# Gate rows ahead of the attention's operands, retention chunks behind it, and more buffers for the merge and the output weight

## The chip, the cores and the metric

The kernel runs on one NeuronCore of a Trainium2 chip. The metric is the device time of one execution in microseconds (us); lower is better. A profile shows one execution with the start, the length and the releaser of each instruction on TensorE (PE), VectorE (DVE), ScalarE (ACT), GpSimd (POOL) and the DMA queue of SyncE (SP).

## The reference

One step of a decoder layer: sparse attention (an indexer picks up to 256 keys for each token) beside multi-scale retention, both gated and merged, for 1024 tokens of a prompt and 32 tokens of eight sampled sequences (4 each). All arithmetic is in float32. What matters here comes behind the projection `u = h @ w_in`:

```python
y_a = attn_fn(qa, ka, va, qi, ki, wi) * silu(za)          # 1056 x 512
y_r = group_norm_heads(ret) * g_ret * silu(zr)            # 1056 x 512
merged = sigmoid(ga) * (y_a @ w_pa) + sigmoid(gr) * (y_r @ w_pr)   # 1056 x 1024
x = x + gate[:, None, :] * (merged @ w_out)               # 1056 x 1024
y = rms_norm(x, g_final)
```
The outputs are y, the new rows of keys, values and indexer keys, and the retention states.

## The kernel before

The arrays are held with channels on the partitions and tokens along the row: a row tile is 128 channels by TT = 1056 tokens (1024 prompt, 32 sample). To keep float32 precision each product of a big matrix is done as three matmuls, high part by high part, high by low and low by high. `parts` splits a row: ACT copies it to the high part (L829) and DVE takes the difference as the low part (L830). A weight is split in the same way by `wsplit` (ACT `wh` L194, DVE or POOL `wl` L195).

The projection, the indexer and the choice of keys fill the first 830 us. What follows goes in four stages.

1. *Retention's inputs and the gates* (to 855): `rows_in` reads the four rows of y_r back from the DRAM tensor YR by way of a buffer `u` and splits them into `rh`, `rl`. The gates, as tanh rows in DRAM (TG: rows 0 to 1023 for the attention, 1024 to 2047 for the retention; (1 + tanh)/2 is the sigmoid), are finished.
2. *Attention of the prompt, with the retention's product beside it* (855 to 1025). There are 16 steps: four pairs of heads `p`, two groups of blocks of 128 tokens, two halves. `pair_operands` loads a pair's q, kh, kl (twelve loads of 64 rows, two heads), V and za. `logits` makes a step's logits (L1055, L1056) and the softmax (DVE L1057, ACT L1062, POOL L1064); `turn` transposes the weights (L1077, copies L1079); `combine` multiplies by V (L1094) and, with every second step, scales by za and splits into `yah`, `yal`. Step s + 2's logits are made behind step s's combination. Beside it `from_retention(j)` yields, for each block j of 128 output channels (0 to 7), three *chunks* c of 352 tokens: 12 matmuls each (4 blocks of 128 input channels by 3), written in one bank of PSUM (`out_weights`, L875 to L877). `use_r` scales a chunk by its gate row `u` (L1118). After the third chunk the row is stored to the DRAM tensor RT (L1120). The list `side` holds all 24 chunks; 9 are drawn at the first step and one at each of the others.
3. *Merge* (1025 to 1077). For each j the gate row `t` (from TG, L1172) and the retention's row `u` (from RT, L1173) are loaded; 12 matmuls for each of three chunks of `yah`, `yal` by `w_pa`; `use_a` scales by the gate (DVE L1176), adds the retention (POOL L1177) and splits the sum into MH and ML (the last 32 tokens into MS). The tile's release on DVE frees the bank for a later chunk; there are four banks (`pj`, bufs=4). After every second j, `load_wo` loads 128 columns of the first half of `w_out` into `wst` (L1163), ACT writes the high part `woh` (L1165), POOL or DVE the low part `wol` (L1166).
4. *Output* (1077 to the end). The other half of `w_out` is loaded in the same way in a pool `op_` that opens when the merge's rows are closed, and the product MH, ML by WO goes over nine tiles of tokens with two halves of columns (L1215 to L1225), followed by the gate, the residual and the norm.

Engines work off their instructions in order. The program's text gives the order only roughly: a scheduler with a model of the times (`schedule_with_timeline_sim=True`) places the instructions on each engine, and `tc.issue_after(x)` keeps the instructions inside it from being placed ahead of x. Almost all transfers are issued by SP, in its order: a transfer that waits holds the ones behind it. A tile's buffers are given round robin: with bufs=2 the third tile of a name waits until the users of the first are done. Pools whose memory overlaps that of a closed pool wait for that pool's last users as well (`reuse_waits="tile"`: tile by tile); `side="right"` allots from the other end of SBUF.

Of the kernel before, what the change touches and what calls it, by code (L numbers as in the profile page):

```python
# [2 lines left out]

# [5 lines left out]
F32 = mybir.dt.float32  # L9
# [4 lines left out]
OP = mybir.AluOpType  # L14
# [4 lines left out]
D = 1024  # L19
T = 1024  # L20
NB, NI = 8, 4
NS = NB * NI
TT = T + NS
CH = TT // 3
KT = D // 128
# [94 lines left out]
def _hybrid_step(ctx, tc, A, outs, dbg):  # L120
    nc = tc.nc
    f32 = lambda ap: ap.bitcast(F32)

    cst = ctx.enter_context(tc.tile_pool(name="cst", bufs=1, reuse_waits="tile"))
    dram = ctx.enter_context(tc.tile_pool(name="scr", bufs=1, space=DRAM))
    wp_ = ExitStack()
    wp = wp_.enter_context(tc.tile_pool(name="wp", bufs=2, side="right", reuse_waits="tile"))
    selp = ctx.enter_context(tc.tile_pool(name="selp", bufs=1, reuse_waits="tile"))
    hs_ = ExitStack()
    hp = hs_.enter_context(tc.tile_pool(name="hp", bufs=1, reuse_waits="tile", side="right"))  # L130
    ps1 = ExitStack()
# [268 lines left out]
    TG = dram.tile([2 * D, TT], F32, name="TG")  # L400
# [180 lines left out]
    with ExitStack() as s1:  # L581
# [4 lines left out]
        with ExitStack() as s2:  # L586
# [35 lines left out]
            for g in range(3):  # L622
                p = pt().rearrange("p (t c) -> p t c", c=128)
                for t in range(4 * g, min(4 * g + 4, 9)):
                    n = 128 if t < 8 else NS
# [11 lines left out]
            for b in range(7, 1, -1):  # L637
                W = (b + 1) * 128
                for h in range(4):
                    p = pl()  # L640
# [30 lines left out]
            for G in (0, 1):  # L671
                p = pt()[:, :128]
                nc.tensor.matmul(p, SX[:NS, 128 * G:128 * G + 128], dw.rearrange("p h t -> p (h t)"), start=True, stop=True)
                t = ip.tile([128, 4, NS], F32, name="wt", bufs=2)
# [4 lines left out]
            for G in (0, 1):  # L679
                KP = []  # L680
                for b in range(4 * G, 4 * G + 4):
# [5 lines left out]
                    p = pt()  # L687
# [5 lines left out]
                x, xn = pl(), pt()  # L693
# [12 lines left out]
            x, xn = pl(), pt()  # L706
# [120 lines left out]
    def parts(dst, src):  # L827

        nc.scalar.copy(dst[0], src)  # L829
        nc.vector.tensor_sub(dst[1], src, f32(dst[0]))  # L830
# [37 lines left out]
    def out_weights(src, use, j, kt, rows_h, rows_l):  # L868

        wh, wl = wsplit(wq, wload(wq, src, 128 * j, 128, kt), 128, kt)  # L870
        for c in range(3):
            x = pj()[:, :CH]
            sl = slice(c * CH, c * CH + CH)
            for k in range(kt):
                nc.tensor.matmul(x, wh[:, k], rows_h[:, k, sl], start=(k == 0), stop=False)  # L875
                nc.tensor.matmul(x, wh[:, k], rows_l[:, k, sl], start=False, stop=False)  # L876
                nc.tensor.matmul(x, wl[:, k], rows_h[:, k, sl], start=False, stop=(k == kt - 1))  # L877
            use(c, sl, x)
            yield

    def rows_in(pool, src):
        hi, lo = [pool.tile([128, 4, TT], F32R, name=n) for n in ("rh", "rl")]
        for k in range(4):
            t = pool.tile([128, TT], F32, name="u", bufs=2)
            nc.sync.dma_start(t, src[128 * k:128 * k + 128])
            parts((hi[:, k], lo[:, k]), t)
        return hi, lo
# [101 lines left out]
    for p in range(4):  # L989
        x = tl.tile([128, TT], F32, name="kx", bufs=1)  # L990
        split_rows(tl, O_KA + 128 * p, p, KD, ks, x)
        token_rows(tl, x, p, k_out, ks_out, None)
    for p in range(4):
        x = tl.tile([128, TT], F32, name="raw", bufs=2)
# [8 lines left out]
    rm = rm_.enter_context(tc.tile_pool(name="rm", bufs=1, reuse_waits="tile"))  # L1003
# [12 lines left out]
    yah, yal = [yp.tile([128, 4, TT], F32R, name=n) for n in ("yah", "yal")]  # L1016
# [24 lines left out]
    def logits(ap, step):  # L1041

        blocks, ops = step["blocks"], step["ops"][0]
        lg = step["lg"] = ap.tile([128, 2, 9 * 128], F32, name="lg", bufs=3)
        c0 = 0
        for b in blocks:
            W = (b + 1) * 128
            for i, (q, kh, kl) in enumerate(ops):
                l = lg[:, i, c0:c0 + W]
                st = ap.tile([128, 4], F32, name="st", bufs=12)  # L1050
                qb = q[:, b * 128:b * 128 + 128]
                for n0 in range(0, W, 512):
                    n1 = min(W, n0 + 512)
                    x = pbank("lg", 2)
                    nc.tensor.matmul(x[:, :n1 - n0], qb, kh[:, n0:n1], start=True, stop=False)  # L1055
                    nc.tensor.matmul(x[:, :n1 - n0], qb, kl[:, n0:n1], start=False, stop=True)  # L1056
                    nc.vector.tensor_tensor_reduce(  # L1057
                        out=l[:, n0:n1], in0=x[:, :n1 - n0], in1=BI[b][:, n0:n1], scale=1.0,
                        scalar=BIGNEG if n0 == 0 else st[:, 0:1], op0=OP.add, op1=OP.max,
                        accum_out=st[:, 0:1] if n1 < W else st[:, 1:2])  # L1060
                nc.vector.tensor_scalar(st[:, 2:3], st[:, 1:2], -0.125, None, op0=OP.mult)  # L1061
                nc.scalar.activation(l, l, AF.Exp, bias=st[:, 2:3], scale=0.125, accum_out=st[:, 3:4])  # L1062
                nc.vector.reciprocal(st[:, 0:1], st[:, 3:4])  # L1063
                nc.gpsimd.tensor_scalar(l, l, st[:, 0:1], 0.5, op0=OP.mult, op1=OP.mult)  # L1064
            c0 += W
# [37 lines left out]
    RT = dram.tile([D, TT], F32, name="RT")  # L1103
    with ExitStack() as s4:
        ap = s4.enter_context(tc.tile_pool(name="ap", bufs=1, side="right", reuse_waits="tile"))
        loaded = {}

        def operands(p):
            if p not in loaded:
                loaded[p] = pair_operands(ap, p)  # L1110
            return loaded[p]

        def from_retention(j):
            u = rm.tile([128, TT], F32, name="u", bufs=2)
            nc.sync.dma_start(u, TG[D + 128 * j:D + 128 * j + 128])

            def use_r(c, sl, x):
                nc.vector.scalar_tensor_tensor(u[:, sl], u[:, sl], 1.0, x, op0=OP.add, op1=OP.mult)  # L1118
            yield from out_weights(A["w_pr"][0], use_r, j, 4, yrh, yrl)
            nc.sync.dma_start(RT[128 * j:128 * j + 128], u)  # L1120

        steps = []
        for p in range(4):
            for group in ((7, 0, 6, 1), (5, 2, 4, 3)):
                po = [None]
                for half in (0, 1):
                    steps.append(dict(p=p, group=group, blocks=group[2 * half:2 * half + 2], half=half, po=po))
        side = (x for j in range(KT) for x in from_retention(j))
        for s_, step in enumerate(steps[:2]):
            step["ops"] = operands(step["p"])  # L1130
            logits(ap, step)
        for s_, step in enumerate(steps):
            turn(ap, step)
            if s_ % 4 == 0 and step["p"] + 1 < 4:
                operands(step["p"] + 1)
            combine(ap, step)
            if s_ + 2 < len(steps):
                steps[s_ + 2]["ops"] = operands(steps[s_ + 2]["p"])
                logits(ap, steps[s_ + 2])
            with tc.issue_after(steps[s_ - 1]["last"].ins) if s_ else nullcontext():  # L1140
                for _ in zip(range(1 if s_ else 9), side):
                    pass
        for _ in side:
            pass
    rm_.close()
# [9 lines left out]
    fp = ctx.enter_context(tc.tile_pool(name="fp", bufs=1, reuse_waits="tile"))  # L1155
    MH, ML = [fp.tile([128, KT, T], F32R, name=n) for n in ("MH", "ML")]
    MS = fp.tile([128, KT, 2, NS], F32R, name="MS")
    WO = [[fp.tile([128, KT, 512], F32R, name=f"wo{a}0") for a in "hl"]]

    def load_wo(q, js):  # L1160
        for j in js:
            w = fp.tile([128, KT, 128], F32, name="wst", bufs=2)
            nc.sync.dma_start(w, wcols(A["w_out"][0], KT, 512 * q + 128 * j, 128))  # L1163
            sl = slice(128 * j, 128 * j + 128)
            nc.scalar.copy(WO[q][0][:, :, sl], w)  # L1165
            (nc.vector if j % 2 else nc.gpsimd).tensor_tensor(WO[q][1][:, :, sl], w, f32(WO[q][0][:, :, sl]), op=OP.subtract)  # L1166

    with ExitStack() as s5:
        mp = s5.enter_context(tc.tile_pool(name="mp", bufs=1, reuse_waits="tile"))
        for j in range(KT):  # L1170
            t, u = [mp.tile([128, TT], F32, name=n, bufs=2) for n in "tu"]
            nc.sync.dma_start(t, TG[128 * j:128 * j + 128])  # L1172
            nc.sync.dma_start(u, RT[128 * j:128 * j + 128])  # L1173

            def use_a(c, sl, x):
                nc.vector.scalar_tensor_tensor(t[:, sl], t[:, sl], 1.0, x, op0=OP.add, op1=OP.mult)  # L1176
                nc.gpsimd.tensor_tensor(t[:, sl], t[:, sl], u[:, sl], op=OP.add)  # L1177
                end = min(sl.stop, T)
                parts((MH[:, j, sl.start:end], ML[:, j, sl.start:end]), t[:, sl.start:end])
                if c == 2:  # L1180
                    parts((MS[:, j, 0], MS[:, j, 1]), t[:, T:])
            for _ in out_weights(A["w_pa"][0], use_a, j, 4, yah, yal):
                pass
            if j % 2 == 1:
                load_wo(0, (j // 2,))
    yp_.close()

    op_ = ctx.enter_context(tc.tile_pool(name="op", bufs=1, reuse_waits="tile"))
    WO.append([op_.tile([128, KT, 512], F32R, name=f"wo{a}1") for a in "hl"])
# [89 lines left out]
```

## Time and profile before

| | us |
|---|---|
| median of 3 runs | 1189.28 (1185.84 to 1189.39) |
| profiled execution | 1189.59 |
| its span | 1187.8 (mean granted TensorE clock 0.972) |
| PE busy | 1108.8 (93%) |
| DVE, ACT, POOL busy | 664.8, 454.3, 329.7 |
| attention and retention's product | 855 to 1025.45 |
| merge | 1025.45 to 1077.05 |
| output product | 1077.05 to 1179.70 |

A row of the waits view reads: engine and line, what it waited for, the time in total, how often, the longest. A row of the chain reads: start, length, what; the chain is followed back from the last instruction to what released each step. A row of the windows reads: the stretch, its length, busy time of each engine with the number of instructions, the granted clock of TensorE (1.00 is full), the busy share of the 16 DMA engines, and GB/s.

### The profile page before, as it was taken

What the parts mean: (1) busy time and instruction counts of PE and PEld (TensorE: products, weight loads), DVE (VectorE), ACT (ScalarE), POOL (GpSimd) and SP (SyncE); (2) the same over time, 40 slices, a digit from 0 to 9 for tenths busy, and PEclk for the clock granted to TensorE, in tenths of its full rate; (3) what the DMA queues carried; (4) which work ended last, traced back from release to release, by engine and by line L of the source; (5) the groups of instructions that cost most, each with busy time, mean ns of one, the idle gap of its engine ahead of it and who ended that gap; (6) DMA issues with size and microseconds to landing.
All of it is one profiled execution on the core that took longest, in us unless ns stands there. A gap on an engine that the chain in (4) does not pass through costs nothing. (4 is left out here: it accounts for less than half of the span.)

```text
span 1187.8 us, 20303 instructions
## 1 busy us (share of the span) xinstructions
PE 1108.8 (93%) x8040; PEld 1011.9 (85%) x8040; DVE 664.8 (56%) x1599; ACT 454.3 (38%) x874; POOL 329.7 (28%) x258
## 2 busy tenths in 40 slices
PE   4999999999989959999998999999997999988997
PEld 3899989999889959999998999777976888886786
DVE  6765359999999996023222122100364766586655
ACT  5365455554555202122233332211343656432211
POOL 3413016024212511241321212242132333484000
PEclk9899999999999978999999999999998999999999
DMA  9913244144224323332775776687898551586221
GB/s 308 244 35 105 73 122 129 26 151 119 74 78 127 110 57 113 93 106 65 265 252 177 223 215 185 198 287 245 243 246 230 156 159 46 161 248 186 96 104 54
DMA packets 157892, 181.51 MB, mean 153 GB/s; under 512 B 18837, under 2 KB 129501, under 8 KB 156710
## 3 DMA queue, kind: packets, MB, share of 16 engines
q1 hardware_dynamic: 147864, 144.51, 41.5%
q0 software_dynamic: 9856, 35.66, 9.2%
q8 instruction: 63, 1.03, 0.4%
q14 instruction: 31, 0.25, 0.1%
q10 hardware_dynamic: 78, 0.06, 0.0%
HBM read 137.81 MB, written 38.60 MB: 149 GB/s over the span
## 5 line engine op out<-in xcount | busy, mean ns | idle before, releaser
L208 PE MATMUL pj<-hh,wh 128*128 128x352 f32 x1176 | 387.9, 330 | 8.7 <-ACT kx L394 3.7
L210 PE MATMUL pj<-hh,wl 128*128 128x352 f32 x1176 | 382.8, 325 | 0.0
L209 PE MATMUL pj<-hl,wh 128*128 128x352 f32 x1176 | 382.7, 325 | 0.0
L208 PEld LDWEIGHTS pj<-hh,wh 128*128 128x128 f32 x1176 | 223.0, 190 | 18.5 <-issue 6.4
L210 PEld LDWEIGHTS pj<-hh,wl 128*128 128x128 f32 x1176 | 223.2, 190 | 3.9 <-issue 3.4
L209 PEld LDWEIGHTS pj<-hl,wh 128*128 128x128 f32 x1176 | 223.6, 190 | 3.3 <-issue 2.5
L727 DVE TENSOR_SCALAR_CACHE_REDUCE eq<-sc,cand 128x896 bf16<-128x896 f32 (+4 forms) x155 | 135.7, 876 | 2.3
L195 POOL TENSOR_TENSOR wl<-ws,wh 128x1024 fp32r<-128x1024 f32 (+1 forms) x33 | 65.1, 1973 | 187.7 <-ACT wh L194 187.7
L194 ACT CAST wh<-ws 128x1024 fp32r<-128x1024 f32 (+1 forms) x65 | 61.2, 942 | 102.8 <-PE pj L209 66.3
L195 DVE TENSOR_TENSOR wl<-ws,wh 128x1024 fp32r<-128x1024 f32 x32 | 40.0, 1250 | 87.1 <-ACT wh L194 81.2
L1064 POOL TENSOR_SCALAR lg<-lg,st 128x1024 f32<-128x1024 f32 (+7 forms) x64 | 47.4, 746 | 93.4 <-DVE st L1063 83.9
L1062 ACT ACTIVATE lg<-lg,st 128x1024 f32<-128x1024 f32 (+7 forms) x64 | 49.5, 774 | 34.4 <-DVE st L1061 34.1
L734 ACT ACTIVATE ra<-sc,cand 128x1024 bf16<-128x1024 f32 x31 | 35.7, 1151 | 65.1 <-DVE cand L805 65.1
L910 POOL DMA_INDIRECT kv<-in_cache_k,idx x32 | 30.9, 965 | 102.8 <-PE str L940 84.7
L942 DVE COPY kt<-str 128x512 f32<-128x512 f32 x32 | 22.1, 690 | 61.0 <-PE str L940 53.8
L910 POOL DMA_INDIRECT kv<-in_cache_v,idx x32 | 31.7, 992 | 72.4 <-PE sx L968 43.3
L1215 PE MATMUL pj<-woh,MH 128*128 128x512 f32 (+1 forms) x136 | 51.5, 380 | 0.0
L1217 PE MATMUL pj<-woh,ML 128*128 128x512 f32 (+1 forms) x136 | 51.2, 377 | 0.0
L1216 PE MATMUL pj<-wol,MH 128*128 128x512 f32 (+1 forms) x136 | 51.2, 377 | 0.0
L573 ACT ACTIVATE raw<-pj 128x352 f32<-128x352 f32 x48 | 22.1, 460 | 72.5 <-PE pj L210 65.6
L1077 PE MATMUL tr<-C,lg 128*128 128x128 f32 x288 | 43.6, 275 | 0.8 <-DVE pT L1079 0.3
L1057 DVE CUSTOM_DVE_ANT_0 lg<-lg,bi 128x512 f32<-128x512 f32 (+3 forms) x64 | 37.1, 587 | 9.0 <-PE lg L1056 8.4
(337 smaller groups left out, 2054.4 us busy)
## 6 DMA issues: line engine op xcount, KB each, us to landing
ws<-in_w_in SPq DMA_DIRECT2D x51, 512.0 KB
TG<-raw SPq DMA_DIRECT2D x16, 528.0 KB
rot<-in_rot SPq DMA_DIRECT2D x8, 1056.0 KB
wa<-in_w_ada SPq DMA_DIRECT2D x16, 512.0 KB
u<-TG SPq DMA_DIRECT2D x8, 528.0 KB
RT<-u SPq DMA_DIRECT2D x8, 528.0 KB
t<-TG SPq DMA_DIRECT2D x8, 528.0 KB
u<-RT SPq DMA_DIRECT2D x8, 528.0 KB
```

Source lines behind the costliest of these rows:

```text
L194: nc.scalar.copy(wh[:, :, :n], ws[:, :, :n])
L195: (nc.vector if len(order) % 3 else nc.gpsimd).tensor_sub(wl[:, :, :n], ws[:, :, :n], f32(wh[:, :, :n]))
L208: nc.tensor.matmul(p, wh[:, k], HH[k][:, sl], start=(k == 0), stop=False)
L209: nc.tensor.matmul(p, wh[:, k], HL[k][:, sl], start=False, stop=False)
L210: nc.tensor.matmul(p, wl[:, k], HH[k][:, sl], start=False, stop=(k == KT - 1))
L727: nc.vector.tensor_scalar(junk[:n, :W], sc, thr[:n, j:j + 1], 0.0, op0=op, op1=OP.add, accum_out=cnt[:n, j:j + 1])
L910: nc.gpsimd.indirect_dma_start(out=t.rearrange("p s c -> p (s c)"), out_offset=None, in_=cache.rearrange("g (r s) h d -> (g r) (s h d)", s ...
L1062: nc.scalar.activation(l, l, AF.Exp, bias=st[:, 2:3], scale=0.125, accum_out=st[:, 3:4])
L1064: nc.gpsimd.tensor_scalar(l, l, st[:, 0:1], 0.5, op0=OP.mult, op1=OP.mult)
L1215: nc.tensor.matmul(x, MH[:, k, tk], wh[:, k], start=(k == 0), stop=False)
L1216: nc.tensor.matmul(x, MH[:, k, tk], wl[:, k], start=False, stop=False)
L1217: nc.tensor.matmul(x, ML[:, k, tk], wh[:, k], start=False, stop=(k == KT - 1))
```

## The change

- The buffer `u` of the pool `rm` has three instead of two copies. The gate rows of j = 0, 1 and 2 are loaded ahead of the first pair's operands (`load_gate`), and that of j + 2 when block j begins (j = 1 to 5).
- The nine chunks that are drawn first come ahead of the first `turn`; one is drawn in each of the steps 0 to 11, and the last three behind the last step's combination.
- The operands of the next pair may be placed only behind the load of gate row 3 (`issue_after(asked[3])`).
- The pool `mp` of the merge's rows `t` and `u` is opened on the other side, before the last chunks, and the rows of j = 0 and 1 are asked for there. To make place, the pool `selp` (the attention's bias rows) goes to that side as well and is closed after the merge.
- `wst`, the landing buffer of the output weight, has four instead of two copies.

```diff
--- before.py
+++ after.py
@@ -1,5 +1,5 @@
 import math
-from contextlib import ExitStack, nullcontext
+from contextlib import ExitStack
 
 import numpy as np
 import concourse.bass as bass
@@ -123,9 +123,10 @@
 
     cst = ctx.enter_context(tc.tile_pool(name="cst", bufs=1, reuse_waits="tile"))
     dram = ctx.enter_context(tc.tile_pool(name="scr", bufs=1, space=DRAM))
+    sel_ = ExitStack()
+    selp = sel_.enter_context(tc.tile_pool(name="selp", bufs=1, side="right", reuse_waits="tile"))
     wp_ = ExitStack()
     wp = wp_.enter_context(tc.tile_pool(name="wp", bufs=2, side="right", reuse_waits="tile"))
-    selp = ctx.enter_context(tc.tile_pool(name="selp", bufs=1, reuse_waits="tile"))
     hs_ = ExitStack()
     hp = hs_.enter_context(tc.tile_pool(name="hp", bufs=1, reuse_waits="tile", side="right"))
     ps1 = ExitStack()
@@ -881,7 +882,7 @@
     def rows_in(pool, src):
         hi, lo = [pool.tile([128, 4, TT], F32R, name=n) for n in ("rh", "rl")]
         for k in range(4):
-            t = pool.tile([128, TT], F32, name="u", bufs=2)
+            t = pool.tile([128, TT], F32, name="u", bufs=3)
             nc.sync.dma_start(t, src[128 * k:128 * k + 128])
             parts((hi[:, k], lo[:, k]), t)
         return hi, lo
@@ -1110,15 +1111,24 @@
                 loaded[p] = pair_operands(ap, p)
             return loaded[p]
 
+        gate, asked = {}, {}
+
+        def load_gate(j):
+            gate[j] = rm.tile([128, TT], F32, name="u", bufs=3)
+            asked[j] = nc.sync.dma_start(gate[j], TG[D + 128 * j:D + 128 * j + 128])
+
         def from_retention(j):
-            u = rm.tile([128, TT], F32, name="u", bufs=2)
-            nc.sync.dma_start(u, TG[D + 128 * j:D + 128 * j + 128])
+            if 0 < j < KT - 2:
+                load_gate(j + 2)
+            u = gate[j]
 
             def use_r(c, sl, x):
                 nc.vector.scalar_tensor_tensor(u[:, sl], u[:, sl], 1.0, x, op0=OP.add, op1=OP.mult)
             yield from out_weights(A["w_pr"][0], use_r, j, 4, yrh, yrl)
             nc.sync.dma_start(RT[128 * j:128 * j + 128], u)
 
+        for j in range(3):
+            load_gate(j)
         steps = []
         for p in range(4):
             for group in ((7, 0, 6, 1), (5, 2, 4, 3)):
@@ -1129,17 +1139,32 @@
         for s_, step in enumerate(steps[:2]):
             step["ops"] = operands(step["p"])
             logits(ap, step)
+        for _ in zip(range(9), side):
+            pass
         for s_, step in enumerate(steps):
             turn(ap, step)
             if s_ % 4 == 0 and step["p"] + 1 < 4:
-                operands(step["p"] + 1)
+                with tc.issue_after(asked[3].ins):
+                    operands(step["p"] + 1)
             combine(ap, step)
             if s_ + 2 < len(steps):
                 steps[s_ + 2]["ops"] = operands(steps[s_ + 2]["p"])
                 logits(ap, steps[s_ + 2])
-            with tc.issue_after(steps[s_ - 1]["last"].ins) if s_ else nullcontext():
-                for _ in zip(range(1 if s_ else 9), side):
+            with tc.issue_after(steps[max(s_ - 1, 0)]["last"].ins):
+                for _ in zip(range(int(s_ <= 11)), side):
                     pass
+        last = steps[-1]["last"]
+    mp_ = ExitStack()
+    mp = mp_.enter_context(tc.tile_pool(name="mp", bufs=1, side="right", reuse_waits="tile"))
+    merged = {}
+
+    def load_merged(j):
+        merged[j] = [mp.tile([128, TT], F32, name=n, bufs=2) for n in "tu"]
+        nc.sync.dma_start(merged[j][0], TG[128 * j:128 * j + 128])
+        nc.sync.dma_start(merged[j][1], RT[128 * j:128 * j + 128])
+    load_merged(0)
+    load_merged(1)
+    with tc.issue_after(last.ins):
         for _ in side:
             pass
     rm_.close()
@@ -1159,31 +1184,31 @@
 
     def load_wo(q, js):
         for j in js:
-            w = fp.tile([128, KT, 128], F32, name="wst", bufs=2)
+            w = fp.tile([128, KT, 128], F32, name="wst", bufs=4)
             nc.sync.dma_start(w, wcols(A["w_out"][0], KT, 512 * q + 128 * j, 128))
             sl = slice(128 * j, 128 * j + 128)
             nc.scalar.copy(WO[q][0][:, :, sl], w)
             (nc.vector if j % 2 else nc.gpsimd).tensor_tensor(WO[q][1][:, :, sl], w, f32(WO[q][0][:, :, sl]), op=OP.subtract)
 
-    with ExitStack() as s5:
-        mp = s5.enter_context(tc.tile_pool(name="mp", bufs=1, reuse_waits="tile"))
-        for j in range(KT):
-            t, u = [mp.tile([128, TT], F32, name=n, bufs=2) for n in "tu"]
-            nc.sync.dma_start(t, TG[128 * j:128 * j + 128])
-            nc.sync.dma_start(u, RT[128 * j:128 * j + 128])
-
-            def use_a(c, sl, x):
-                nc.vector.scalar_tensor_tensor(t[:, sl], t[:, sl], 1.0, x, op0=OP.add, op1=OP.mult)
-                nc.gpsimd.tensor_tensor(t[:, sl], t[:, sl], u[:, sl], op=OP.add)
-                end = min(sl.stop, T)
-                parts((MH[:, j, sl.start:end], ML[:, j, sl.start:end]), t[:, sl.start:end])
-                if c == 2:
-                    parts((MS[:, j, 0], MS[:, j, 1]), t[:, T:])
-            for _ in out_weights(A["w_pa"][0], use_a, j, 4, yah, yal):
-                pass
-            if j % 2 == 1:
-                load_wo(0, (j // 2,))
+    for j in range(KT):
+        if j not in merged:
+            load_merged(j)
+        t, u = merged[j]
+
+        def use_a(c, sl, x):
+            nc.vector.scalar_tensor_tensor(t[:, sl], t[:, sl], 1.0, x, op0=OP.add, op1=OP.mult)
+            nc.gpsimd.tensor_tensor(t[:, sl], t[:, sl], u[:, sl], op=OP.add)
+            end = min(sl.stop, T)
+            parts((MH[:, j, sl.start:end], ML[:, j, sl.start:end]), t[:, sl.start:end])
+            if c == 2:
+                parts((MS[:, j, 0], MS[:, j, 1]), t[:, T:])
+        for _ in out_weights(A["w_pa"][0], use_a, j, 4, yah, yal):
+            pass
+        if j % 2 == 1:
+            load_wo(0, (j // 2,))
+    mp_.close()
     yp_.close()
+    sel_.close()
 
     op_ = ctx.enter_context(tc.tile_pool(name="op", bufs=1, reuse_waits="tile"))
     WO.append([op_.tile([128, KT, 512], F32R, name=f"wo{a}1") for a in "hl"])
```

Behind the change the lines of the profile move: L1118 becomes L1126, L1120 becomes L1128, L1163 to L1166 become L1188 to L1191, L1172 and L1173 become L1163 and L1164, L1176 and L1177 become L1199 and L1200; the helpers from L829 to L1106 move by one.

## The prediction

> **What bounds the kernel now.** I read the page first, then PE's waits over the stages that the change touches (855 to 1100), then windows around each long wait, then the chain inside them.
>
> ```profile
> span 1187.8 us, 20303 instructions
> PE 1108.8 (93%) x8040; PEld 1011.9 (85%) x8040; DVE 664.8 (56%) x1599; ACT 454.3 (38%) x874; POOL 329.7 (28%) x258
> ```
> ```profile
> engine line waited for: us in total, times, longest us
> PE pj L875 <- DVE u L1118: 7.3, 1, 7.3
> PE pj L1225 <- ACT woh L1165: 4.4, 1, 4.4
> PE pj L875 <- DVE t L1176: 2.8, 1, 2.8
> PE lg L1056 <- DMA kl<-kdl: 1.5, 1, 1.5
> ...
> PE pj L1222 <- DVE wol L1166: 0.7, 1, 0.7
> ```
> TensorE is the bound: 1108.8 of 1187.8 us. It multiplies as much after the change as before, so only its waits, and the clock that it loses by them, can move the time. The list gives three waits in the changed stages: A (7.3, retention's product), C (2.8, merge) and D (4.4, output product). The windows give their places and what follows each:
>
> ```profile
> core 0: us, PE busy (x) PEld busy (x) DVE busy (x) ACT busy (x) POOL busy (x), PEclk, DMA share, GB/s
> 855.00:890.98 35.98, 33.17 (x219) 28.73 (x218) 19.08 (x76) 15.13 (x36) 11.46 (x14) 1.00 1.00 238
> 890.98:898.25 7.27, 0.00 (x1) 0.01 (x1) 0.58 (x2) 0.00 (x0) 0.00 (x0) 0.69 1.06 345
> 898.25:903.84 5.59, 5.59 (x30) 5.21 (x32) 2.16 (x11) 2.25 (x5) 1.78 (x3) 0.50 0.89 213
> 1016.43:1025.45 9.02, 8.21 (x100) 7.38 (x99) 1.29 (x3) 3.34 (x7) 2.61 (x3) 1.00 0.25 89
> 1051.40:1054.23 2.83, 0.01 (x1) 0.00 (x0) 2.83 (x3) 0.62 (x1) 2.83 (x2) 0.98 0.91 260
> 1054.23:1057.76 3.53, 3.52 (x13) 3.53 (x13) 2.82 (x5) 0.97 (x2) 3.53 (x4) 0.53 1.13 313
> 1091.81:1096.20 4.39, 0.00 (x0) 0.00 (x1) 0.38 (x1) 2.09 (x2) 2.34 (x1) 0.87 1.11 277
> 1096.20:1101.80 5.60, 4.94 (x12) 2.31 (x13) 5.06 (x7) 1.11 (x3) 0.00 (x0) 0.50 0.20 79
> ```
> After each wait PE runs at a granted clock of about half (0.50, 0.53, 0.50). What that costs is read from one matmul of the same product at either clock:
>
> ```profile
> 874.58 0.16 PE pj L877
> ...
> 883.77 8.81 DMA RT<-u
> ...
> 892.60 4.98 DMA u<-TG
> ...
> 897.67 0.53 DVE u L1118
> ...
> 1051.12 2.63 DVE ML L830
> ...
> 1054.89 0.29 PE pj L876
> ```
> 0.16 becomes 0.29 us, so 45% of the busy time at the low clock is lost: 2.5 of 5.59 after A, 1.6 of 3.52 after C, 2.2 of 4.94 after D. With the idle time A costs 9.8, C 4.4, and D 7.3 (its 4.39, the 0.7 of the fifth line of waits, and 2.2).
>
> **The change, part by part.** The sum is made against the profiled execution: 1189.59 us, 1.8 above its span and 0.3 above the median of 1189.28.
>
> *Three gate rows (A).* Row j=2 of the retention's gate has to take one of two buffers, so its load waits until j=0's product has been stored: the chain shows the store in the queue behind the second pair's operands for 8.81 us, the row 4.98 more, and PE standing behind the scaling at L1118. With three buffers rows 0 to 2 are loaded ahead of every operand, and the first nine chunks (a chunk is 12 matmuls and 352 columns, a third of a block j) need no store. A goes: -9.8. What is late next is row j=3, whose load waits for the store of j=0. The third chunk ends at 874.74 (the first chain row is its last matmul). With L1118's 0.53 and, as an upper bound, another 8.81 in the queue, the store lands by 884.1, and the row another 4.98 later, 889.1. Chunk 9 is after the ninth chunk and the first combination, near 887 once A is gone, and the banks of PSUM let PE run on a little while the scaling is late. The row will not be that late, because the queue ahead of the store no longer holds all of the second pair. I take nothing, and up to 4 for the range. The wait of 1.5 on `kl` stays.
>
> *Last three chunks behind the attention.* They move 3 x 2.0 us of matmuls from before the end of the attention (P, 1025.45) to behind it. The conservation is exact; what is lost is filler. In the last window ahead of P, which still held a chunk, PE stood idle 0.81 of 9.02. Four steps now lack theirs: between 0 and 4 x 0.81 = 3.2. DVE and ACT were busy 1.29 and 3.34 of 9.02 there, so they don't become the bound; I take +1.5. P comes at -9.8 + 1.5 - 5.9 = 14.2 earlier.
>
> *Merge (C).* This is where the change can give time back.
>
> ```profile
> 1025.45:1077.05 51.60, 48.41 (x289) 47.30 (x289) 39.27 (x53) 18.84 (x39) 36.16 (x29) 0.97 0.80 250
> 1028.00:1048.00 20.00, 19.64 (x122) 19.06 (x121) 14.45 (x20) 8.50 (x16) 14.22 (x12) 1.00 0.96 303
> 1040.00:1060.00 20.00, 16.81 (x93) 15.95 (x93) 16.40 (x20) 7.19 (x15) 15.70 (x12) 0.91 0.93 281
> ```
> ```profile
> 1026.21 0.32 SPq L1172
> ...
> 1026.58 4.80 DMA u<-RT
> ```
> C itself came from VectorE, which worked off an output weight (its load, ACT's `woh`, DVE's `wol`) and an ML of 2.63 us ahead of the scaling that frees PE's bank. In the changed order these weights stand later on DVE, behind j=0 and 1, whose rows SP issues ahead of the retention's last store; so C as it is goes, -4.4. But DMA was busy 0.96 of the window 1028 to 1048: this stage is close to the limit of SP's transfers too. The order of instructions of the changed kernel shows what SP issues behind P: rows 0 and 1 early; then the store of the retention's last block, which waits for the moved chunks; only then a `ws`, **four** `wst` of 512 KB at once (four buffers), a `ws`, u2 and t2; then `wst`, `wst`, u3, `ws`, `wst`, t3; then `wst`, `ws`, u4, t4. Behind P, PE does two retention chunks, the first of the merge, the last of the retention, then the merge alone. A merge chunk is (51.60 - 2.83 - 1.6)/24 = 1.97 us, so the last retention chunk ends at P + 7.9 and SP is free at P + 8.6 (with 0.53 of scaling). Four banks of PSUM let PE go on without a row until chunk 9 ends, P + 25.7, for t2 (chunk 6's bank is wanted), P + 31.6 for t3, P + 37.5 for t4, each later by what was lost before.
>
> Up to t2 stand 4.24 MB (the store and two rows of 0.541 each, two `ws` of 0.262, four `wst` of 0.524); up to t3 2.92 MB more; up to t4 1.87 more. Two rows (1.08 MB) came in 5.2 us in the rows above, 3.6 of it at 303 GB/s, so 1.6 is fixed. At 281 GB/s t2 lands at 8.6 + 15.1 + 1.6 = P + 25.3 (in time), t3 at P + 35.7 (4.1 late), t4 at P + 42.4 (0.8 late): 4.9 idle. At 303 it is 2 idle, at 250, the mean of the whole stage, 1.3 + 5.8 + 1.5 = 8.6. The rate nearest in load is the middle one, measured with `wst`, `ws` and rows mixed, so 4.9. The clock: the idle 1.5 of `kl` lies in the first window, whose clock is 1.00, and cost none, one of 2.83 cost 1.6, so 4.1 in one piece costs about 1.8. Bounds: 2 and 11.6, taken 6.7. The Trainium skill, TensorE: Matmul & The Clock Gate, section on the HAM clock gate, has the array throttled after an idle window of about 3.4 us; the row of 2.83 with 0.53 behind it shows that less can do. By the page's figure alone the 303 GB/s case would keep its clock, and the middle one would not.
>
> Behind P there are 27 chunks, 53.2, and 6.7 of waits: 59.9 against 51.6, +8.3. The end of the merge comes at -14.2 + 8.3 = -5.9.
>
> *Output weights with four buffers (D).*
>
> ```profile
> 1083.69 2.01 ACT woh L1165 x2
> 1085.72 2.65 DVE wol L1166
> 1088.39 0.41 SPq L1163
> ```
> Halves 2 and 3 of the second `w_out` block could only be loaded at 1088.39, when the first two had left the two buffers, and these had waited until the last MS. With four buffers all four lie there before the merge ends: their places in SP's order are ahead of t5. Four `woh` of 1.0 (half of 2.01) on ACT and two `wol` on each of DVE and POOL (2.65) then take some 8 us from the last MS, against PE's need 14.8 us after the merge's end (1077.05 to 1091.81). D goes: -7.3.
>
> **Sum:** 1189.6 - 9.8 + 1.5 (tail) + 6.7 - 4.4 - 7.3 = 1176.3; the chunk counts of the two sides cancel but for 0.4 in rounding. I predict 1176.
>
> **Rivals.**
> 1. *Only the gains* (0.18). The rows t2 and t3 come in time: 1189.6 - 9.8 + 1.5 - 4.4 - 7.3 = 1169.6. For it: 345 GB/s was moved in the window of A. It needs 7.16 MB in 31.6 - 8.6 - 1.6 = 21.4 us, 335 GB/s; against it, no window of the merge had more than 313.
> 2. *A deeper backlog* (0.17): at 250 GB/s or with each of t2 to t5 late, 11.6 instead of 6.7 or a few more: 1181 to 1185.
> 3. *The output weights stay late* (0.07). The change does not do what it says if the second block's loads still wait for buffers that ACT, behind the rows' rounding, empties late. D stays: 1183.6.
> 4. *Slower: SP stands behind gate row 3* (0.05). The second pair's operands may now be issued only after the load of row j=3, which waits for the store of j=0. If that landed late, PE would have no logits for the fifth step.
>
> ```profile
> 916.76 0.48 PE L1055 MATMUL lg<-kh,qd 128*128 128x512 f32 x1
> ```
> That step's first logits run at 916.76 in the profile (behind the third combination), so at 907.0 without A. From 884.1, the row and six operand loads (0.54 and 6 x 0.262 MB) at the 238 GB/s of the first window end at 894.6 with the fixed 1.6. So there are 12.4 us of room, and each further one counts in full. To lose the 13.3 gained and 3.6 more, the operands would have to be 29.3 us later, at 924: only if SP waited for a second and a third store too. The Trainium skill, DMA: Bandwidth & Descriptors, section on queues, rings and completion order, has SP own a single row of queues, consumed in ring order: a held SP holds all of these transfers, rows, operands and weights alike; the 8.81 of the store is that in this trace.
> The forecast keeps 0.53.
>
> **How the numbers follow.** About 0.3%, 3.6 us, is what a measurement of this kernel can tell from no change. The forecast, rivals 1 and 3, and most of 2 lie below 1185.7: 0.90 faster. The same, 0.06: the far end of the backlog together with 3, or a small part of 4. Slower, 0.04: the rest of 4. The range goes from a little under rival 1 (no loss in the tail, 1168) to rivals 2 and 3, 1185.
>
> **What would show it.** Right: no wait for L1118's successor near 890 and a clock of 1.0 there; the last combination some 14 us earlier; PE's longest wait in the merge on the scaling of t (rows t2 or t3, DMA `t<-TG` or `u<-RT` behind), with half the clock after it; none on `woh` in the output stage. Wrong in size: the merge without a wait (1170), or with over 9 us of them (over 1180). Wrong in kind: a wait on `kh`, `kl` or `qd` after 890, a wait on the gate row of j=3 or later, or `woh` still waited for.

## The result

The changed kernel takes 1171.01 us (median of 4 runs, 1169.86 to 1172.77) against 1189.0 for the kernel before (4 runs, 1185.84 to 1189.39): a ratio of 0.9856, 95% interval 0.9833 to 0.9878. Forecast were 1176.0, 1168 to 1185. Its profiled execution took 1169.95, with a span of 1168.1.

The waits of PE from 850 to 1100 in the changed kernel (engine and line, what it waited for, total, times, longest):

```profile
PE pj L876 <- DVE t L1199: 2.7, 1, 2.7
PE lg L1057 <- DMA kl<-kdl: 1.4, 1, 1.4
PE pj L878 <- POOL wl L196: 1.2, 1, 1.2
```
The 7.3 on the retention's scaling (A) and the 4.4 on `woh` (D) are gone. The wait in the merge on the scaling of t, 2.8 before (C), stands there with 2.7 as if nothing had been done, and one of 1.2 on a split weight has joined it.

Three stages tell where the time went. They are cut at the retention's first matmul, at the end of the last attention product (P) and at the merge's last matmul; the third stage runs to the end of the span. Before, then after (stretch, its length, busy time of PE, PEld, DVE, ACT, POOL, clock, DMA share, GB/s):

```profile
854.95:1025.45 170.50, 158.69 (x1346) 140.61 (x1345) 101.83 (x384) 89.02 (x198) 57.53 (x72) 0.97 0.58 158
1025.45:1077.21 51.76, 48.57 (x289) 47.41 (x290) 39.30 (x53) 18.84 (x39) 36.16 (x29) 0.97 0.80 249
1077.21:1187.80 110.59, 97.40 (x441) 77.88 (x438) 61.62 (x153) 19.92 (x48) 7.75 (x5) 0.95 0.31 104
```
```profile
852.36:1007.17 154.81, 150.29 (x1310) 131.60 (x1309) 100.14 (x381) 87.01 (x197) 56.26 (x71) 1.00 0.62 169
1007.17:1064.99 57.82, 53.90 (x326) 53.24 (x326) 41.68 (x56) 19.47 (x40) 38.07 (x30) 0.97 0.78 245
1064.99:1168.10 103.11, 94.97 (x441) 77.03 (x438) 63.86 (x155) 19.62 (x48) 8.75 (x5) 0.98 0.27 102
```
The first stage lost 15.7 (of these some 6.0 are the three chunks, of 2.0 each, that went behind P, so 9.7 in waits and filler) and its clock is 1.00 where it was 0.97. The merge took 6.1 longer, the three chunks, so its waits gave nothing back. The output stage lost 7.5. The remaining 2.6 of the 19.7 between the two spans lie ahead of the first row. The change touches little there (the side of `selp`, the third buffer `u` in `rows_in`), and the place of that row differs from one profiled execution to the next, between 851.3 and 855.7 over all kernels here, also among those that are alike up to it. So the experiments below are compared by these three lengths, each from one profiled execution, and by ratios with their intervals. Each ratio is to runs of the kernel before that were taken together with the row's own (their medians are 1188.5 to 1191.1), so ratios can be compared from row to row more safely than medians.

| kernel | median us (runs) | ratio to before, 95% interval | to P | merge | output |
|---|---|---|---|---|---|
| before | 1189.0 (4) | | 170.5 | 51.8 | 110.6 |
| changed | 1171.0 (4) | 0.9856 (0.9833 to 0.9878) | 154.8 | 57.8* | 103.1 |
| e1_gate_rows | 1179.1 (6) | 0.9919 (0.9890 to 0.9949) | 160.2 | 53.2 | 109.8 |
| e2_wst2 | 1175.3 (6) | 0.9891 (0.9866 to 0.9917) | 155.2 | 56.8* | 108.5 |
| e3_chunks_in_steps | 1168.9 (6) | 0.9839 (0.9814 to 0.9865) | 159.6 | 52.9 | 103.3 |
| e4_before_wst3 | 1185.6 (12) | 0.9971 (0.9954 to 0.9987) | 170.3 | 53.6 | 108.4 |
| e5_no_asked | 1179.6 (6) | 0.9914 (0.9891 to 0.9938) | 161.6 | 59.6* | 103.2 |
| e6_wo_late | 1170.5 (6) | 0.9856 (0.9832 to 0.9880) | 154.9 | 56.0* | 103.2 |
| e7_wo_both | 1168.4 (6) | 0.9828 (0.9802 to 0.9854) | 154.7 | 54.1* | 103.7 |
| e8_rows_first | 1172.5 (5) | 0.9847 (0.9831 to 0.9863) | 154.8 | 59.7* | 103.0 |
| e9_wol_dve | 1172.9 (6) | 0.9861 (0.9839 to 0.9884) | 154.7 | 57.8* | 103.4 |
| e12_rows_steps | 1171.8 (5) | 0.9831 (0.9809 to 0.9854) | 159.5 | 53.5 | 103.0 |
| e14_late_rows3 | 1168.9 (5) | 0.9813 (0.9788 to 0.9837) | 155.1 | 55.7* | 102.9 |
| e15_late_steps_rows3 | 1166.8 (5) | 0.9797 (0.9780 to 0.9814) | 159.7 | 46.6 | 103.0 |

\* with three chunks of the retention, 6.0 us, that the others have ahead of P.

### The profile page after: what moved, and what is told of

Its sections match the earlier page's. It is cut to its first block, busy times and chain, and to the rows that moved or that the text cites. A ratio compares the mean times of both kernels' runs of the same rounds, so it can differ in the third digit from the quotient of the medians.

```text
span 1168.1 us, 20306 instructions
## 1 busy us (share of the span) xinstructions
PE 1104.2 (95%) x8040; PEld 1008.5 (86%) x8040; DVE 669.1 (57%) x1599; ACT 452.8 (39%) x874; POOL 329.6 (28%) x258
## 5 line engine op out<-in xcount | busy, mean ns | idle before, releaser
L195 ACT CAST wh<-ws 128x1024 fp32r<-128x1024 f32 (+1 forms) x65 | 61.1, 940 | 108.4 <-PE pj L210 66.9
L1078 PEld LDWEIGHTS tr<-C,lg 128*128 128x128 f32 x288 | 33.7, 140 | 8.7 <-ACT pT L1080 1.9
```

What stands on the lines that cost most here:

```text
L195: nc.scalar.copy(wh[:, :, :n], ws[:, :, :n])
L1078: nc.tensor.transpose(x[:, 128 * (j - j0):128 * (j - j0) + 128], lg[:, j % 2, 128 * (j // 2):128 * (j // 2) + 128], ident)
```

## The experiments

### The gate rows alone (e1)

The kernel before, with `load_gate`, three buffers u, nine chunks ahead and `issue_after(asked[3])` from the change, and

```diff
-            with tc.issue_after(steps[s_ - 1]["last"].ins) if s_ else nullcontext():
-                for _ in zip(range(1 if s_ else 9), side):
+            with tc.issue_after(steps[max(s_ - 1, 0)]["last"].ins):
+                for _ in zip(range(1), side):
```


> The kernel before with the first part of the change alone: three buffers u, gate rows 0 to 2 loaded ahead of the operands, nine chunks ahead of the first turn, operands of the next pair behind gate row 3; one chunk in each of the 15 further steps, merge and output as before. Theory (the prediction's part A): the wait of 7.3 on the scaling and the half clock behind it go, 9.8 to 11 us, waits C (2.8) and D (4.4) stay: 1178 to 1179.5. Rival: a wait on gate row 3 or on the second pair's operands takes its place: 1183 or more.

1179.1: the first stage fell by 10.3, and the other two waits stayed. PE's waits from 870 to 1110 in it:

```profile
PE pj L1237 <- ACT woh L1177: 4.7, 1, 4.7
PE pj L875 <- DVE t L1188: 3.5, 1, 3.5
PE lg L1056 <- DMA kl<-kdl: 1.6, 1, 1.6
```
Part A was priced at 9.8. No new wait took its place.

### The order of the second pair's operands (e5)

```diff
-                with tc.issue_after(asked[3].ins):
-                    operands(step["p"] + 1)
+                operands(step["p"] + 1)
```


> The changed kernel without the order that holds the second pair's operands behind gate row 3: the first six of them now stand in SP's order ahead of the store of j = 1 and of gate row 3. Theory (the prediction's rival 4 in reverse): PE waits for the weights or gate row of chunk 9 or later, 3 to 7 us with half the clock: 1174 to 1180. Rival (there is room on both sides, so the order costs and gains nothing): 1170 to 1172.

1179.6: the first stage is 6.8 longer than in the changed kernel, and the merge 1.8. PE waits at a combination, not at chunk 9's weights or row as expected. The chain ahead of PE's wait of 5.0 in it (start, length, what):

```profile
867.18 10.23 DMA qd<-qdl
...
877.43 9.52 DMA u<-TG
...
887.01 9.18 DMA ws<-in_w_pr
...
896.27 0.12 ACT wh L195
...
896.80 0.38 ACT pT L1080
...
897.22 0.90 PE po L1095 x5
```
Row j=3 and behind it the weight `ws` of a next block wait in SP's queue beside the operands, 9 us each; ACT, which works in order, stands at that weight's split and so delivers the copy `pT` late, for which the combination waits. What the prediction had as a danger (SP held behind gate row 3) is what keeps A from coming back with another name: 6.8 of the 15.7 that the first stage gained.

### The buffers of the output weight (e2, e4)

The changed kernel with two buffers, and the kernel before with three (four don't fit beside its other tiles):

```diff
-            w = fp.tile([128, KT, 128], F32, name="wst", bufs=4)
+            w = fp.tile([128, KT, 128], F32, name="wst", bufs=2)
```


> The changed kernel with two buffers wst instead of four. Theory (part D): the wait on woh in the output stage returns, 7.3 us with its half clock: 1178. If SP's four weights ahead of row t2 are what PE pays for in the merge, the merge's waits (3.9 idle in the changed kernel) shrink at the same time and it comes out near 1173 to 1175; if VectorE's order is what PE pays for, they stay or move with the place of wol on VectorE.

> The kernel before with three buffers wst instead of two (four do not fit beside its other tiles). Theory (part D): one of the two late halves of the second w_out block is loaded early, so the wait on woh in the output stage shrinks or goes, and what is left is a wait on the fourth half: 3 to 7 of the 7.3 us: 1182 to 1186. Waits A and C stay. Rival (the wait is on ACT and GpSimd, not on the buffer): 1188 to 1190.

With two, the output stage is 108.5 against 103.1, and PE waits there for both parts of the late half (rows of e2, PE's waits):

```profile
PE pj L1250 <- ACT woh L1190: 2.3, 1, 2.3
PE pj L876 <- DVE t L1199: 2.3, 1, 2.3
PE pj L1247 <- DVE wol L1191: 1.5, 1, 1.5
```
5.4 came back, not 7.3 or 7.5. The wait in the merge became 2.3, with 1.1 more on `wl`. It begins 29.7 behind P instead of 26.5, and VectorE's `wol` (2.64, beside one on GpSimd) stands ahead of it there: with two weights ahead in SP's queue instead of four it did not go, it moved with the `wol`. In the kernel before, a third buffer took 2.2 off the output stage and put 1.8 on the merge, whose waits on t rose from 2.8 to 4.2: a weight that comes earlier has its `woh` and `wol` done earlier, in the merge. The trace has GpSimd's second `wol` there at 17.2 behind P (24.6 before), with an ML of 2.65 beside it ahead of the scaling that PE waits for. The ratio is 0.9971, some 3.4 us; the three lengths of the one profiled execution leave 0.6, so part of it is not in that trace.

### Chunks behind P or not (e3)

```diff
-                for _ in zip(range(int(s_ <= 11)), side):
+                for _ in zip(range(1), side):
```


> The changed kernel with a chunk in each step, so none is left behind the last combination; the rest as changed. Theory (the prediction's tail term): P comes 5.9 later less about 1.5 of idle that the chunks fill, the merge is 5.9 shorter: 1169.5 to 1171. Rival: moving the chunks behind P is what gives the rows and weights time, so the merge's waits grow without it: 1173 or more.

To P 159.6, that is 153.6 without the three chunks, against 154.8: the filler is worth 1.2 (1.5 in the prediction). The merge gives it back: 52.9, against 51.8 without the chunks in the changed kernel, for the wait on t is 4.4 there instead of 2.7. Moving the chunks by itself does nothing that these runs can tell: the two stages together are 212.5 and 212.6, and the intervals of the two ratios overlap.

### What stands in the merge (e6, e7, e9)

Two theories. The prediction's: rows t2 and t3 land late, behind the four weights in SP's queue. The other comes from the changed kernel's chain (start, length, what) and from VectorE's timeline ahead of PE's wait:

```profile
1020.08 7.78 DMA wst<-in_w_out
...
1027.88 1.06 ACT woh L1190
...
1028.97 1.70 DVE wol L1191
1030.67 1.76 DVE ML L831 x2
...
1034.68 1.25 DVE MS L831
1035.93 0.44 DVE t L1199
...
1036.41 0.47 PE pj L876
```
```profile
1030.60 4.17 DVE L831 TENSOR_TENSOR ML<-t,MH 128x352 fp32r<-128x352 f32 x2
1034.68 1.25 DVE L831 TENSOR_TENSOR MS<-t,MS 128x32 fp32r<-128x32 f32 x1
1035.85 1.37 DVE L1199 SCALAR_TENSOR_TENSOR t<-t,pj 128x352 f32<-128x352 f32 x3
```
VectorE does not wait for a row there. It is busy from 1030.60 to the scaling with two ML in 4.17 and an MS of 1.25, having done two `wol` just before. GpSimd runs beside them:

```profile
1031.76 2.65 POOL L1191 TENSOR_TENSOR wol<-wst,woh 128x1024 fp32r<-128x1024 f32 x1
1034.38 1.51 POOL L196 TENSOR_TENSOR wl<-ws,wh 128x512 fp32r<-128x512 f32 x1
```
The second ML took 2.66 beside the `wol`, the MS 1.25 beside the `wl`. This is the picture of C, which had one `wol` and one ML of 2.63 on VectorE.

e6 puts VectorE's `wol` later, e7 those of VectorE and GpSimd; SP's four `wst` stay ahead of t2 in both. e7:

```diff
+    seen, WHEN = {}, {3: (0,), 4: (1,), 5: (2,), 6: (3,)}
...
-            nc.vector.scalar_tensor_tensor(t[:, sl], ...)
-            nc.gpsimd.tensor_tensor(t[:, sl], t[:, sl], u[:, sl], op=OP.add)
+            seen[j] = [nc.vector.scalar_tensor_tensor(t[:, sl], ...),
+                       nc.gpsimd.tensor_tensor(t[:, sl], t[:, sl], u[:, sl], op=OP.add)]
...
-        if j % 2 == 1:
-            load_wo(0, (j // 2,))
+        if j in WHEN:
+            with tc.issue_after(seen[j][0].ins), tc.issue_after(seen[j][1].ins):
+                load_wo(0, WHEN[j])
```
(e6 has `issue_after` for VectorE's instruction alone.) In e9 all four `wol` of the first half are on VectorE, at early places:

```diff
-            (nc.vector if j % 2 else nc.gpsimd).tensor_tensor(WO...
+            (nc.vector if j % 2 or q == 0 else nc.gpsimd).tensor_tensor(WO...
```


> The changed kernel with the two wol of the first half that VectorE does placed behind the scalings of j = 3 to 6; SP's order up to row t2 (four wst ahead of it) and GpSimd's order are those of the changed kernel. Theory 1 (VectorE's order: wol and ML stand ahead of the scaling of j = 2): PE's wait of 2.7 on the scaling and the 1.7 lost at half clock go, the 1.2 on GpSimd's wl stays: 1166 to 1167.5. Theory 2 (the prediction's: row t2 or t3 lands late behind the weights): the wait stays, with DMA t<-TG ahead of it: 1170 to 1172.

> The changed kernel with the low parts wol of the first half placed behind the merge's j = 3 to 6 on VectorE and on GpSimd; SP still issues the four wst ahead of row t2. Theory 1 (what stands ahead of the scaling of j = 2 on VectorE is stretched by GpSimd's wol beside it: ML 2.5 and MS 1.25 us there, 0.5 and 0.18 alone): the merge's waits at j = 2 (2.7) and on wl (1.2) go, the stretch from the last attention product to the end of the merge falls from 57.8 to 53 or 54. Theory 2 (rows behind the weights in SP's queue): a wait on row t2 or t3 of 2 us or more remains: 56 or more.

> The changed kernel with all four wol of the first half on VectorE, at their early places, none on GpSimd. Theory 1 (GpSimd beside VectorE is what stretches ML and MS): with two wol more (3 us) on VectorE, but ML at 0.5 to 0.8 us, the wait at j = 2 is under 1.5 and that on wl is gone: the merge's stretch falls from 57.8 to 55 or less. If it is the sheer number of VectorE's operations ahead of the scaling, the wait grows by the two wol, to 4 or 5 us: 59 or more. Theory 2 (rows late): unchanged, 57 to 58.

e6: the two `wol` of VectorE were gone from that place, and the wait was not (2.70). Two ML still took 4.02 and the MS 1.25 there, beside GpSimd's `wol` and `wl`. (The 1.2 on `wl` went, which was not expected, and 0.8 on t came at the end.) The scaling came 1.4 earlier, 27.3 behind P instead of 28.7, but so did PE, which had not waited for `wl`. So VectorE's own `wol` are not enough to explain the wait; theory 2's number came out for the total, but not its mark: no row was waited for at the wait. The merge is 1.9 shorter all the same. The largest part of that is the clock, which stayed at 1.00 behind a wait as long as that of the changed kernel, where half the clock cost some 1.7:

```profile
1031.38:1034.08 2.70, 0.00 (x1) 0.00 (x0) 2.70 (x4) 0.00 (x0) 2.17 (x2) 1.00 0.57 195
1034.08:1037.48 3.40, 3.40 (x21) 3.40 (x22) 2.46 (x4) 1.23 (x3) 3.04 (x3) 1.00 0.85 250
```
That is luck, not the edit: see the last section.

e7: with GpSimd's moved too, the same MS takes 0.18 (it had 1.25), with nothing on GpSimd beside it, and the wait at j = 2 is gone. PE's wait in e7's merge, then VectorE's for rows (1010 to 1070):

```profile
PE pj L876 <- DVE t L1200: 1.5, 1, 1.5
```
```profile
DVE t L1200 <- DMA t<-TG: 8.1, 5, 2.8
```
The merge is 54.1 against 57.8, so theory 1 holds for this wait. In the whole time the gain is not clear of noise (the intervals of 0.9828 and 0.9856 overlap). Theory 2's mark is there now, on VectorE: 8.1 of waits for rows. Further on PE waits 1.5, up to 1052, and 0.7 of that is one of them. It was the next bound, hidden behind the first.

e9 contradicts the simple form of theory 1 (GpSimd beside VectorE is all): with no `wol` on GpSimd, the ML of 320 columns took 0.61 on average against 1.02, but four `wol` took 7.5 of VectorE instead of 3.2, and PE waited 2.5 and 1.2. What one side gained the other lost. The work of the `wol` ahead of j = 2's scaling costs PE wherever it is done; moving it behind helps.

### Rows ahead of the weights (e8, e12)

e8 is e7 with SP's order turned round as well (`rows[j]` is the load of u), with the weights at j = 2 to 5; e12 has e3's edit besides.

```diff
-    seen, WHEN = {}, {3: (0,), 4: (1,), 5: (2,), 6: (3,)}
+    seen, WHEN = {}, {2: (0,), 3: (1,), 4: (2,), 5: (3,)}
...
-            with tc.issue_after(seen[j][0].ins), tc.issue_after(seen[j][1].ins):
+            with tc.issue_after(seen[j][0].ins), tc.issue_after(seen[j][1].ins), tc.issue_after(rows[j + 0].ins):
```


> The changed kernel with SP's order in the merge turned round: each wst stands behind a row of RT, so two weights and not four go ahead of row t3, and the wol of the first half follow the scalings of j = 2 to 5 on VectorE and GpSimd. Both theories say that the merge's waits now go: the stretch from the last attention product to the end of the merge is 53 to 54.5 (57.8 in the changed kernel, 54.1 with the late wol alone), and VectorE's waits for rows (8.1 with the late wol alone) fall under 4. Rival: the two last weights of the second half land late, and 1 to 5 us come back in the output stage. In all 1166 to 1168.

> As the run before, and with a chunk in each step of the attention, so none behind it. The idle time of the last steps (1.2 by the two runs that differ in it) goes, and SP is free for the merge from the last combination on. 1164.5 to 1167. Rival: the merge gets the rows later in its own terms (no chunks to wait behind), and a wait of 2 to 4 us on row t2 comes back: 1167 to 1170.

Both expectations missed. The merge took 59.7, longer than in the changed kernel, and 53.5 without the chunks; PE waited 3.0 and 3.9 at about 1054, at the scaling of a later block. Fewer weights ahead of row t3 is not what was wanted. The chain ahead of that wait in e8 (start, length, what):

```profile
1048.82 0.85 DVE MS L831
...
1049.71 5.99 DMA t<-TG
...
1055.82 0.53 DVE t L1200
...
1056.40 0.66 PE pj L876
```
Row t5 could only be asked for when the MS of j = 3 had left the buffer, and then took 6 us to land; e12 shows the same with 6.95. So this wait is for a late row, but one that was asked for late, for want of a buffer. The same holds for t3 in the changed kernel. SP's own rows (start, length, what):

```profile
1026.48 0.34 SPq L1163 DMA_DIRECT2D t<-TG  x1
1026.92 2.27 SPq L1188 DMA_DIRECT2D wst<-in_w_out  x2
1029.61 2.42 SPq L1164 DMA_DIRECT2D u<-RT  x1
1032.12 0.39 SPq L189 DMA_DIRECT2D ws<-in_w_pa  x1
1032.60 0.74 SPq L1188 DMA_DIRECT2D wst<-in_w_out  x1
1035.96 0.34 SPq L1163 DMA_DIRECT2D t<-TG  x1
```
t3 is asked for at 1035.96, when the MS of j = 1 (1034.68 + 1.25) has left its buffer: it waited for VectorE, with SP issuing nothing for 2.6 ahead of it.

### Three buffers for the rows (e14, e15)

e14 is e7 with three buffers for t and u; the third pair of rows then stands ahead of the weights. e15 has e3's edit besides.

```diff
-        merged[j] = [mp.tile([128, TT], F32, name=n, bufs=2) for n in "tu"]
+        merged[j] = [mp.tile([128, TT], F32, name=n, bufs=3) for n in "tu"]
```


> The kernel with the late wol on both engines and, besides, three buffers for the merge's rows t and u: the rows of j = 2 stand ahead of the weights in SP's order, and those of later j no longer wait for the last MS two blocks before. Theory: what is left in the merge with the late wol (PE 1.5 at 1052, VectorE 8.1 for rows) comes from rows that wait for a buffer and then land late; with three it falls to under 3 for VectorE and PE's wait goes: the stretch from the last attention product to the end of the merge is 53.2 to 54 (54.1 with two), in all 1166 to 1168. Rival: four weights at a stretch still stand ahead of row t3 or t4, and a wait of 2 to 4 stays: 55 to 57.

> As the run before, with a chunk in each step of the attention and none behind it: 1.2 us of idle time in the last steps go, 1165 to 1167. Rival: with SP free 8 us earlier but the same order, the merge's row waits grow by what the attention gains: no difference from the run before.

e14: VectorE's waits for rows fell from 8.1 to 1.2, but PE waits 2.1 on t (at 1046), with half the clock behind it: 55.7, no better than e7, and the rival of its expectation. The chain ahead of this wait goes through a row that took 7.1 to land behind the four weights, and then through an ML of 2.26 and an MS of 1.25 beside GpSimd's moved `wol` and its `wl`: both limits again, at a later place. e15: nothing of over 0.3 is left in the merge.

```profile
PE lg L1057 <- DMA kl<-kdl: 1.4, 1, 1.4
PE tr L1078 <- ACT pT L1080: 1.0, 3, 0.4
PE po L1095 <- ACT pT L1080: 0.5, 1, 0.5
PE pj L876 <- DVE t L1200: 0.3, 1, 0.3
```
```profile
1015.39:1062.02 46.63, 46.31 (x289) 45.95 (x290) 37.35 (x51) 18.60 (x39) 37.38 (x29) 1.00 0.86 277
```
PE is busy 46.31 of 46.63 at full clock; the merge has no more waits to give. Expected were 1.2 from the tail; the three stages of the profiled executions gave 4.4 (313.7 to 309.3), the medians 2.1. That the early free queue and the third row buffer work together is my reading and not shown: a run with the late `wol`, the chunks in the steps and two row buffers is missing. e15 has the lowest ratio, 0.9797 (0.9780 to 0.9814), clear of 0.9856 (0.9833 to 0.9878) for the changed kernel, but not of e7 and e14.

## Why the prediction was right, and where not

The direction, the range and two of three parts held; the forecast was 5 too slow.

- *A*: -9.8 forecast, -10.3 measured alone in e1. The cause (row j=2 behind a store, behind operands) is in the chain of the kernel before, and the wait went with it in e1. Row j=3 and the operands were in time, and e5 shows that the new order is the reason.
- *Tail*: +1.5 forecast, 1.2 by e3. To P the sum had -14.2, and it was -15.7: A's 0.5 more, the tail's 0.3 less, and 0.7 by which e3 is shorter than e1, in small waits that the sum left out.
- *C and the merge*: +8.3 forecast, +6.1 measured, and the reason was wrong. The failed step is "so C as it is goes", with the row t3 as what is late next. C stayed: two `wol`, two ML and an MS on VectorE ahead of a scaling, now that of j = 2 instead of j = 3, with ML and MS stretched by GpSimd's `wol` and `wl`. I read from the changed order that the weights stand behind j = 0 and 1, and stopped there; behind j = 1 is exactly ahead of j = 2. The rows were a real limit, but the second one: e7 uncovers it (8.1 on VectorE). There row t2 is scaled 24.4 behind P, as soon as it has landed, and the prediction had it landing at 25.3. But the queue alone did not set this: t2 and t3 are each asked for when an MS on VectorE has left their buffer (t2 in the changed kernel at 1026.48, the MS of j = 0 ends at 1026.45), a step that the prediction left out. The idle time was 3.9 (2.7 and 1.2) against 4.9, so the size came out near for another reason, which is luck. (At 250 GB/s the prediction's three terms should read 1.5, 5.8 and 1.6, in all 8.8 and not 8.6; nothing hangs on it.)
- *The clock*: the wait of 2.7 was followed by half the clock, as forecast, and so cost more than its length. That it was is luck too, since in e6 one of 2.70 kept it:

```profile
1033.70:1036.41 2.71, 0.01 (x1) 0.00 (x0) 2.71 (x4) 0.00 (x0) 2.18 (x2) 1.00 1.00 328
1036.41:1040.10 3.69, 3.69 (x13) 3.69 (x14) 2.62 (x5) 1.54 (x4) 3.01 (x3) 0.54 1.02 301
```
At 45% lost that is 1.7, with 1.8 in the sum.
- *D*: -7.3 forecast, -7.5 measured, and e2 brings 5.4 of it back. The four halves were there in time.
- *Rivals*: 1 (only the gains, 1169.6) has nearly the measured time and not its mechanism, since C's wait is there. 2 did not happen: the merge's waits came to 3.9 idle, and no row was behind them. 3 did not happen. 4 did not happen; its mechanism in reverse did, in e5.
- What is left between 1176.3 and the profiled 1169.95: 1.5 to P, 2.2 in the merge, 0.2 in the output, and 2.6 in front of all of it, which belong to no step.

## What to carry to other kernels

When a change moves work on an in-order engine, ask what comes next behind its new place, not only what it left: a wait on an operation that moved from j = 3 to j = 2 looks like a new cause and is the old one. A buffer that lets transfers start earlier also lets their follow-up work start earlier, so it needs a place for that work where nothing waits; here the merge lost its waits only in e15, with late `wol`, a third row buffer and the chunks in the steps together, while e6, e7, e8, e9, e12 and e14, which each lack some of this, left 1.5 or more at one place. Cut the profile at the stages that the change touches, since the part ahead of them differed by up to 4.4 us between the profiled executions here.

## What the runs showed of the hardware

VectorE's subtractions with two inputs grow beside GpSimd's: the MS of 32 columns took 0.18 us alone and up to 2.39 beside a `wol`. An ML takes 0.5 alone; two of them took 4.17. The stretched ones end with GpSimd's instruction or just behind it: the MS of 2.39 at 1026.45 with a `wol` that ends at 1026.40, the MS of 1.25 at 1035.93 with a `wl` that ends at 1035.89, the ML of 2.66 at 1034.76 with a `wol` that ends at 1034.41. So what these three cost was set by what was left of GpSimd's instruction, not by their own size. The Trainium skill, GPSIMD Engine Reference, section Specifications, says that the two share their interfaces to SBUF, with contention for VectorE's instructions that have two SBUF inputs; these rows agree.

Idle stretches of about 2 us had both outcomes for the clock of the time behind them: 2.14 in e14 was followed by 3.43 us at 0.53, 2.26 in e2 by 3.38 at 1.00.

```profile
1043.73:1045.87 2.14, 0.00 (x1) 0.00 (x0) 2.14 (x4) 0.00 (x0) 2.14 (x3) 0.96 0.19 75
1045.87:1049.30 3.43, 3.43 (x12) 3.43 (x13) 3.26 (x4) 0.97 (x2) 3.43 (x3) 0.53 0.83 242
```
```profile
1037.76:1040.02 2.26, 0.00 (x0) 0.00 (x1) 2.26 (x4) 0.83 (x3) 2.26 (x2) 1.00 0.71 198
1040.02:1043.40 3.38, 3.38 (x20) 3.25 (x21) 3.13 (x6) 1.24 (x3) 3.38 (x4) 1.00 0.96 283
```
The Trainium skill, TensorE: Matmul & The Clock Gate, section on the HAM clock gate, calls the window free-running, which fits that the length alone doesn't decide; that it takes a whole idle window of about 3.4 us does not fit 2.14, nor the 2.71 of the changed kernel. Among the single idle stretches of over 1 us between 852 and 1120 in all these traces, the shortest with a low clock behind it is 1.56 (0.61 over the next 3.40, in e4), and the longest without is the 2.70 of e6; 1.59 in e1 and 1.70 in e5 were followed by 1.00. Each one from 2.71 on was followed by 0.58 or less. So here a stall of 1.6 to 2.7 us has to be priced with a chance, not with a rule.
